# Some float32r operands begin 64 bytes past a multiple of 128 instead of at one

## The chip, the cores and the metric

The kernel runs as one program on one core of a Trainium2 chip. The metric is the device time of one execution in microseconds (us); the median of several executions is what counts. TensorE (PE) does the matrix products, its weight loads are listed on their own as PEld, VectorE is DVE, ScalarE is ACT, GpSimd is POOL, and SP issues the transfers from HBM.

## The reference, cut to what matters

Two blocks of two layers each work on 256 tokens of width 1024, all in float32:

```python
# first block, layer i = 0, 1
h = mixer_block(h, ...)          # rmsnorm, u @ w_in (1024 x 9232), retention, gated delta rule, two branches, w_out
u = rmsnorm(h, norm_ffn[i])
h = h + swiglu(u, ...)           # layer 0: (silu(u @ wg) * (u @ wu)) @ wd, width 2816
h = h + moe(u, ...)              # layer 1: 8 experts of width 1408, two for each token
h = h + sigmoid(rmsnorm(h, norm_ple[i]) @ w_ple_gate[i]) * (p[i] @ w_ple[i])
# second block, layer 0: hgrn2 mixer, layer 1: dilated attention, each followed by
u = rms_norm(h, norm_g[layer, 2]) * (1.0 + sc2) + sh2
y = swiglu_ffn(u, ffn_w_in[layer], ffn_w_out[layer])     # width 2816
```

Nearly all arithmetic is a product of normed activations with a weight matrix that is read once.

## The kernel before, in words

Each float32 product is made of three float32r products. A value is split into a high part, rounded to float32r, and a low part, the rest; `high*high`, `high*low` and `low*high` are summed in PSUM. For the weights, `fetch` brings 1 MB (128 partitions x 2048 floats) into a buffer `raw`, ACT writes the high part `whi` and DVE the low part `wlo` (`parts`, lines 241 to 263 of the file), two tiles of 1024 columns of each. For the activations, `norm` writes `uh` and `ul`, which live in the constant pool for the whole program and hold 8 blocks of 256 tokens; `split_out` writes the others: `ro` (retention output), `go` (delta-rule output), `ma` (the merged branches), `fh`/`fl` (the hidden layer of a dense FFN), `ho`, `ao`, and in the experts `x`, `y`, `hh`, `hl`.

There are two forms of the product. In `ws_block` the weights are the stationary operand (128 x 128) and the activations move, 256 columns (256 tokens) at a time: three matmuls for each of the 8 blocks of the inner dimension. In `ts_tile` a 128 x 128 block of the activations is stationary and the weights move, 256 columns in `tok` and `toks`, 272 in `gdn_gates`, 384 or 512 in the output projections and the experts. The trace names the moving operand first and the stationary one second: `pg<-uh,whi` is a matmul into `pg` that moves `uh` over the stationary `whi`. Every matmul has a weight load of its own. The order of PE's instructions is the order in which the program is written (a manual schedule for PE); the other engines are ordered by the planner, and a matmul waits only for its operands and for its PSUM tile.

Where a tile lies is decided by the order of first use. A pool is a stretch of each partition's SBUF; inside it every tag gets its buffers at the place where the tag is first asked for, rounded to 32 bytes. The class `Even` wraps a pool: it counts the bytes given so far (`at`) and, before a new tag of type float32r (or one of a few float32 tags that share their place with one), it inserts an unused tile `pad`, so that the tag begins at a multiple of 128 bytes. It pads the end of each pool in the same way, so the next pool begins at a multiple of 128. In the kernel before, the addresses (bytes within a partition) come out so:

| tile | address | modulo 128 | modulo 256 |
|---|---|---|---|
| `h` (8192 bytes, ends at 27840) | 19648 | 64 | 192 |
| `uh`, `ul` (8192 bytes each) | 27904, 36096 | 0 | 0 |
| last tile of the constant pool, 64 bytes | 50016 | 96 | 96 |
| `raw` (3 x 8192 bytes), then `whi`, `wlo` (4 x 4096 bytes each) | 50176, 74752, 91136 | 0 | 0 |
| `go`, four buffers in the mixer's pool | 128512 and up (layer 1: 151552) | 0 | 0 |
| `ro`, `ma`, two shared buffers of the tag `A` | 212096, 220288 | 0 | 128 |
| `fh`, `fl` in the dense FFN | 134656, 157184 | 0 | 0 |
| `ho` and `ao` | 169344 and up, 185984 and up | 0 | 128 |

A block of the inner dimension is 1024 bytes of `uh` and 1024 bytes of a weight tile with 256 columns, so within a tile all operands begin at the same place modulo 256. The one exception is `gdn_gates` (output `pgz`): its weight tile has 272 columns, 1088 bytes, so of the two blocks in a tile the first begins at 0 and the second at 64 modulo 128.

Of the kernel before, what the change touches and what calls it, by code (L numbers as in the profile page):

```python
# [7 lines left out]
F32 = mybir.dt.float32  # L8
F32R = mybir.dt.float32r
# [35 lines left out]
class Even:  # L45
# [3 lines left out]
    def __init__(self, pool, bufs):  # L49
        self.pool, self.bufs, self.at, self.tags, self.pads = pool, bufs, 0, set(), 0  # L50

    def even(self):
        if self.at % 128:
            n = (128 - self.at % 128) // 4
            self.pads += 1
            self.pool.tile([128, n], F32, tag=f"pad{self.pads}", name="pad", bufs=1)
            self.at += 4 * n

    def tile(self, shape, dt, tag=None, name=None, bufs=None):
        if tag is None:  # L60
            tag = name
        if tag not in self.tags:
            if dt == F32R or tag in ("raw", "rawo", "uq", "A", "y", "whi", "wlo"):
                self.even()
            self.tags.add(tag)
            size = 2 if dt == BF16 else 4
            for n in shape[1:]:
                size *= n
            self.at += -(-size // 32) * 32 * (bufs or self.bufs)
        return self.pool.tile(shape, dt, tag=tag, name=name, bufs=bufs or self.bufs)  # L70


@contextmanager
def even_pool(tc, name, bufs, **k):
    with tc.tile_pool(name=name, bufs=bufs, **k) as pool:
        p = Even(pool, bufs)
        yield p
        p.even()
# [6 lines left out]
class Net:  # L85
# [23 lines left out]


    @contextmanager
    def phase(self, name, n, nsplit=0):

        tp = lambda name, bufs: even_pool(self.tc, name, bufs, reuse_waits="tile")
        with ExitStack() as st:
            self.php = pool = st.enter_context(tp(name, 1))
            if n:
                self.ap = st.enter_context(tp(name + "_a", n))
            if nsplit:
                st.enter_context(self.more_weights(0, nsplit))  # L120
            yield pool
# [21 lines left out]
            self.tick()  # L143

    def A(self, name, dt=F32):
        return self.ap.tile([128, 2048], dt, tag="A", name=name)

    def psm(self, name="pm"):
        return self.mm.tile([128, 512], F32, tag="mm", name=name)
# [29 lines left out]
    def setup(self, p):  # L179
        nc = self.nc  # L180
        i = self.i
        self.cst = self.cp.tile([128, NCONST, 128], F32, name="cst")
        nc.sync.dma_start(self.cst[:, 0, :], i["cst"][:, 0, :])
        self.ident = self.cst[:, C_ID, :]
        self.M = self.cst[:, C_M, :]
        self.nhalf = self.cp.tile([128, 16], F32, name="nhalf")
        nc.vector.memset(self.nhalf, -0.5)
        self.ones = self.cp.tile([128, 128], F32, name="ones")
        nc.vector.memset(self.ones, 1.0)
        self.h = self.cp.tile([128, 2, D], F32, name="h")  # L190
        self.u = tuple(self.cp.tile([128, 2048], F32R, name=n) for n in ("uh", "ul"))

    def columns(self, items, new):

# [261 lines left out]
    def mixer(self, l, nxt):  # L456
# [2 lines left out]
        w = self.w3(i["w_in"][l])  # L459
        rq, rk, rv, rg, gq, gk, gv, gz, mgr, mgg = 0, 512, 1024, 2048, 3072, 4096, 5120, 6144, 7184, 8208  # L460
        u, tile = self.next
        with self.phase("mix", 2) as mp:
            self.mp = mp
            self.hold = True
            ret_a = self.pair("ro")
# [184 lines left out]
    def gdn_chain(self, l, p, qkv, st):  # L650

        mp = self.mp
        H = 2 * p
        qs, ks, vs = qkv
        pn = self.pss("pn")
        for j, x in enumerate((qs, ks)):
            sq = mp.tile([128, 2, T], F32, tag="cacc", name="sq2", bufs=2)
            self.act(sq, x, AF.Square)
            yield
            yield  # L660
            for h in range(2):
                for t in range(2):
                    n = t * 4 + j * 2 + h
                    self.mmul(pn[:, n:n + 1], sq[:, h, t * 128:(t + 1) * 128], self.ones[:, 0:1])
        ms = mp.tile([128, 2, 2, 2], F32, tag="gms", name="gms", bufs=2)
        r = mp.tile([128, 2, 2, 2], F32, tag="grn", name="grn", bufs=2)
        self.ts(ms.rearrange("p a b c -> p (a b c)"), pn[:, :8], 4 * EPS, None, OP.add)
        self.pow(r.rearrange("p a b c -> p (a b c)"), ms.rearrange("p a b c -> p (a b c)"), 8)
        hv = mp.tile([128, 2, 2], F32, tag="ghv", name="ghv", bufs=2)
        self.stt(hv, ms[:, :, 1, :], 0.5, r[:, :, 1, :], OP.mult, OP.mult)  # L670
        bp = mp.tile([128, 2, 2], F32, tag="gbp", name="gbp", bufs=2)
        self.tt(bp, r[:, :, 1, :], r[:, :, 1, :], OP.mult)
        self.tt(bp, bp, self.g_beta[:, :, H:H + 2], OP.mult)
        fq = mp.tile([128, 2, 2], F32, tag="gfq", name="gfq", bufs=4)
        self.ts(fq, r[:, :, 0, :], 128.0 ** -0.5)
        uq = mp.tile([128, 1536], F32, tag="uq", name="uq", bufs=4)
        U, Q = (uq[:, 768 * n:768 * (n + 1)].rearrange("p (h n i) -> p h n i", h=2, n=3) for n in range(2))
        pr, dc = {}, {}

        def decay(h):  # L680
            hh = H + h
            pr = self.pss("pr")
            g0 = self.g_g[:, 0, hh:hh + 1].to_broadcast([128, 128])
            g1 = self.g_g[:, 1, hh:hh + 1].to_broadcast([128, 128])
            self.mmul(pr[:, 0:128], g0, self.M, start=True, stop=False)
            self.mmul(pr[:, 0:128], self.idb, self.negb, start=False, stop=True)
            self.mmul(pr[:, 128:384], g1, self.M[:, None, :].to_broadcast([128, 2, 128]))
            self.mmul(pr[:, 256:384], self.idb, self.negb, start=False, stop=True, skip=True)
            dc[h] = mp.tile([128, 3, 128], F32, tag="dc", name="dc", bufs=2)
            for n in range(3):  # L690
                self.act(dc[h][:, n, :], pr[:, n * 128:(n + 1) * 128], AF.Exp, bias=self.g_bias[:, n, hh:hh + 1])

        decay(0)
        pv = self.pss("pv")
        for t in range(2):
            for h in range(2):
                self.tr(pv[:, (t * 2 + h) * 128:(t * 2 + h + 1) * 128], vs[:, h, t * 128:(t + 1) * 128])
        vt = mp.tile([128, 2, 2, 128], F32, tag="vt", name="vt", bufs=4)
        for t in range(2):
            for h in range(2):  # L700
                n = t * 2 + h
                self.act(vt[:, t, h, :], pv[:, n * 128:(n + 1) * 128], AF.Identity, scale=hv[:, t, h:h + 1])
        if p % 2 == 0:
            self.Uc = mp.tile([128, 8, 32], F32, tag="Uc", name="Uc", bufs=2)
        for h in range(2):
            yield
            for x, dst in ((ks, U), (qs, Q)):
                pg = self.pss("pg")
                self.mmul(pg[:, 0:256], ks[:, h, 0:128], x[:, h, :])
                self.mmul(pg[:, 256:384], ks[:, h, 128:256], x[:, h, 128:256])  # L710
                self.stt(dst[:, h, 0:2, :], pg[:, 0:256].rearrange("p (a b) -> p a b", b=128), bp[:, 0, h:h + 1],
                         dc[h][:, 0:2, :])
                self.stt(dst[:, h, 2, :], pg[:, 256:384], bp[:, 1, h:h + 1], dc[h][:, 2, :])
            if not h:
                decay(1)
            for g in range(4):
                r = slice(32 * g, 32 * g + 32)
                n = 4 * (p % 2) + 2 * h
                self.act(self.Uc[r, n:n + 2, :], U[r, h, 0:3:2, r])
        st[p] = U, Q, vt, fq  # L720

    def gdn_out(self, l, st, begun, then, sgz, p, ga):
        mp = self.mp
# [23 lines left out]
        for h in range(2):  # L747
            self.mmul(po[:, h * 128:(h + 1) * 128], Q[:, h, 0, :], z[:, 0, h, :])
            self.mmul(po[:, (2 + h) * 128:(3 + h) * 128], Q[:, h, 1, :], z[:, 0, h, :], start=True, stop=False)
            self.mmul(po[:, (2 + h) * 128:(3 + h) * 128], Q[:, h, 2, :], z[:, 1, h, :], start=False, stop=True)  # L750
        o = mp.tile([128, 1536], F32R, tag="uq", name="go", bufs=4)
        o = o[:, :512], o[:, 512:1024]
        while p not in sgz:
            yield
# [948 lines left out]
def begin(net):  # L1703
# [8 lines left out]
    cols = net.columns([(n, r2(i[n])) for n in ("norm_mix", "norm_ffn", "norm_ple", "ret_gn")],  # L1712
                       lambda: net.tp.tile([128, 512], F32, tag="th", name="colrow", bufs=2)[:, :128])
# [7 lines left out]
    def loads():  # L1721
# [5 lines left out]
        items = [("gdn_gn", i["gdn_gn"]), ("c", r2(i["c"])), ("hgrn_norm_g", r2(i["hgrn_norm_g"])),  # L1727
                 ("lower", r2(i["hgrn_lower_bounds"]))]
        items += [(f"conv{l}", i["conv_w"][l].rearrange("w (r p) -> (w r) p", p=128)) for l in range(2)]
        items += [("ada_b", r2(i["ada_b"])), ("norm_g", i["norm_g"].rearrange("l n (r p) -> (l n r) p", p=128))]  # L1730
        cols = net.columns(items, lambda: net.mp.tile([128, 1536], F32, tag="uq", name="colrow", bufs=4)[:, :128])
        net.dtb, net.nea = [], []
        for l in range(2):
            a = cp.tile([128, 8], F32, name=f"nea{l}")
# [113 lines left out]
```

## Time and the profile before

| | us |
|---|---|
| median of 3 runs (2305.77 to 2308.68) | 2306.74 |
| the profiled execution, its own time | 2304.72 |
| its span, from the first to the last instruction | 2302.8 |
| PE busy | 2230.3 (97%) |
| DVE busy | 1695.0 (74%) |
| ACT busy | 1283.6 (56%) |

A span is one execution as the hardware profiler saw it; the execution's own time holds 1.9 us more around it. Matmuls are pipelined, and each is listed with its latency: one of 256 columns shows 0.28 us although the next begins 0.12 us later. So neither the busy share nor the duration of a matmul tells what it costs; the distance between the starts of successive matmuls does.

### The profile page before, as it was taken

To read this page: it belongs to the slowest core of one execution; us is meant where nothing else is said; L and a number is where in the kernel's file an instruction comes from. 1 tells how busy PE (TensorE), PEld (TensorE's weight loads), DVE (VectorE), ACT (ScalarE), POOL (GpSimd) and SP (SyncE) were. 2 spreads that over 40 slices of the span, in tenths; PEclk is the share of its full clock that TensorE was granted. 3 is DMA by queue.
4 is the path that set the end of the run, shared out by engine and by line. 5 is a ranking of instruction groups with operands and counts; after the bars stand their busy time and mean duration, and the time that the engine had idled before them with its cause. 6 is when DMAs were issued, how large, how long until landed. Compare 5 with 4: busy or idle time off the path is not lost.

```text
span 2302.8 us, 38609 instructions
## 1 busy us (share of the span) xinstructions
PE 2230.3 (97%) x15571; PEld 2070.6 (90%) x15571; DVE 1695.0 (74%) x2596; ACT 1283.6 (56%) x1992; POOL 169.3 (7%) x142
## 2 busy tenths in 40 slices
PE   8999999999999999989999999989999999999998
PEld 7998998998899899978888887887998899998997
DVE  6878667766687885679999997786777666666554
ACT  5655445433566444468787776654543555456443
POOL 0032100000003210000000000331000000000000
PEclk9999999999999999999999999999999999999999
DMA  7443566876454355769999996434677554444553
GB/s 233 147 133 127 185 218 209 280 253 250 150 182 138 103 179 194 245 223 369 318 358 339 319 342 218 131 122 146 229 267 269 198 176 137 149 145 138 182 176 135
DMA packets 338525, 478.57 MB, mean 208 GB/s; under 512 B 9874, under 2 KB 239116, under 8 KB 338340
## 3 DMA queue, kind: packets, MB, share of 16 engines
q1 hardware_dynamic: 338340, 476.05, 61.3%
q8 instruction: 123, 2.02, 0.4%
q14 instruction: 62, 0.51, 0.1%
HBM read 474.95 MB, written 1.06 MB: 207 GB/s over the span
## 4 chain that ended last, share of the span: by engine, by line
issue 31%; PE 20%; DVE 3%; POOL 1%; ACT 1%; POOLq 0%; DVEq 0%; ACTq 0%
PE peg L170 5%; PE peu L170 5%; PE pey L170 5%; DVE wlo L158 1%; PE pgat L170 1%; PE phg L170 1%; PE po L170 1%; PE phq L170 1%; PE pho L170 1%; POOL ms L345 0%; PE psc L170 0%; POOL rs L176 0%; PE pht L173 0%; PE phv L170 0%; ACT whi L155 0%
## 5 line engine op out<-in xcount | busy, mean ns | idle before, releaser
L158 DVE TENSOR_TENSOR wlo<-raw,whi 128x1024 fp32r<-128x1024 f32 (+2 forms) x802 | 929.5, 1178 | 310.3 <-ACT whi L155 303.9
L155 ACT ACTIVATE whi<-raw 128x1024 fp32r<-128x1024 f32 (+3 forms) x828 | 832.6, 1022 | 531.2 <-PE po L170 57.3
L170 PE MATMUL pu<-uh,whi 128*128 128x256 f32 x480 | 136.3, 284 | 0.0
L170 PE MATMUL pg<-uh,whi 128*128 128x256 f32 x480 | 136.0, 283 | 0.0
L170 PE MATMUL pg<-ul,whi 128*128 128x256 f32 x480 | 135.8, 283 | 0.0
L170 PE MATMUL pg<-uh,wlo 128*128 128x256 f32 x480 | 135.8, 283 | 0.0
L170 PE MATMUL pu<-ul,whi 128*128 128x256 f32 x480 | 135.8, 283 | 0.0
L170 PE MATMUL pu<-uh,wlo 128*128 128x256 f32 x480 | 135.8, 283 | 0.0
L345 POOL TENSOR_SCALAR ms<-ss 128x1 f32<-128x1 f32 x30 | 16.4, 548 | 1498.7 <-ACT junk L155 1498.7
L167 DVE SCALAR_TENSOR_TENSOR acc<-raw,cond,acc 128x1024 f32<-128x1024 f32 x84 | 108.3, 1289 | 18.0 <-DMA raw<-in_ada_w_dram 17.2
L170 PE MATMUL paq<-uh,whi 128*128 128x256 f32 x384 | 112.3, 293 | 0.0
L170 PE MATMUL pqkv<-uh,whi 128*128 128x256 f32 x384 | 110.2, 287 | 0.0
L170 PE MATMUL pqkv<-uh,wlo 128*128 128x256 f32 x384 | 108.8, 283 | 0.0
L170 PE MATMUL paq<-uh,wlo 128*128 128x256 f32 x384 | 108.7, 283 | 0.0
L170 PE MATMUL pqkv<-ul,whi 128*128 128x256 f32 x384 | 108.6, 283 | 0.0
L170 PE MATMUL paq<-ul,whi 128*128 128x256 f32 x384 | 108.6, 283 | 0.0
L170 PE MATMUL po<-whi,fh 128*128 128x512 f32 x264 | 103.2, 391 | 1.1 <-DVE fm L167 1.1
L170 PE MATMUL po<-wlo,fh 128*128 128x512 f32 x264 | 103.0, 390 | 0.7 <-DVE wlo L158 0.7
L170 PE MATMUL po<-whi,fl 128*128 128x512 f32 x264 | 102.8, 389 | 0.0
L170 PEld LDWEIGHTS pg<-uh,whi 128*128 128x128 f32 x480 | 92.1, 192 | 0.9 <-ACT fh L155 0.9
L170 PEld LDWEIGHTS pu<-uh,whi 128*128 128x128 f32 x480 | 92.1, 192 | 0.9 <-ACT whi L155 0.9
L170 PEld LDWEIGHTS pg<-uh,wlo 128*128 128x128 f32 x480 | 92.1, 192 | 0.0
(470 smaller groups left out, 6587.6 us busy)
## 6 DMA issues: line engine op xcount, KB each, us to landing
raw<-in_w_in_dram SPq DMA_DIRECT2D x70, 1024.0 KB
raw<-in_ada_w_dram SPq DMA_DIRECT2D x48, 1024.0 KB
raw<-in_ffn_w_in_dram SPq DMA_DIRECT2D x44, 1024.0 KB
raw<-in_attn_w_in_dram SPq DMA_DIRECT2D x36, 1024.0 KB
raw<-in_exp_w_gate_dram SPq DMA_DIRECT2D x32, 1024.0 KB
raw<-in_exp_w_up_dram SPq DMA_DIRECT2D x32, 1024.0 KB
raw<-in_exp_w_down_dram SPq DMA_DIRECT2D x32, 1024.0 KB
raw<-in_ffn_w_out_dram SPq DMA_DIRECT2D x20, 1024.0 KB
```

The source lines that it names most:

```text
L155: self.nc.scalar.activation(out, in_, func, scale=scale, bias=bias, **k)
L158: self.nc.vector.tensor_tensor(out, a, b, op=op)
L167: self.nc.vector.scalar_tensor_tensor(out, a, s, b, op0=op0, op1=op1)
L170: self.nc.tensor.matmul(out, lhsT, rhs, start=start, stop=stop, skip_group_check=skip)
L345: self.nc.gpsimd.tensor_scalar(ms, self.ss[:, t, 0:1], self.ss[:, t, 1:2], EPS, op0=OP.add, op1=OP.add)
```

## The change: what it does, and the diff

`Even.even` and `Even.tile` take a flag `odd`: with it a tag begins at 64 modulo 128 instead of 0. It is set for four tags: `uh` and `ul` in the constant pool, the tag `A` of the mixer's phase (`ro`, then `ma`), and the tag `uq` (`go`, the delta rule's float32 blocks `uq`, and a scratch tile `colrow`). All other tags stay at multiples of 128. The flag is passed through `phase` and kept in `self.odd`, which `A` reads. No instruction is added, removed or reordered by the text of the diff, and no tile changes its size; only pads and addresses change.

```diff
-    def even(self):
-        if self.at % 128:
-            n = (128 - self.at % 128) // 4
+    def even(self, odd=False):
+        n = (64 * odd - self.at) % 128 // 4
+        if n:
             self.pads += 1
             self.pool.tile([128, n], F32, tag=f"pad{self.pads}", name="pad", bufs=1)
             self.at += 4 * n
...
             if dt == F32R or tag in ("raw", "rawo", "uq", "A", "y", "whi", "wlo"):
-                self.even()
+                self.even(odd)
...
-        return self.ap.tile([128, 2048], dt, tag="A", name=name)
+        return self.ap.tile([128, 2048], dt, tag="A", name=name, odd=self.odd)
...
-        self.u = tuple(self.cp.tile([128, 2048], F32R, name=n) for n in ("uh", "ul"))
+        self.u = tuple(self.cp.tile([128, 2048], F32R, name=n, odd=True) for n in ("uh", "ul"))
...
-        with self.phase("mix", 2) as mp:
+        with self.phase("mix", 2, odd=True) as mp:
...
-        uq = mp.tile([128, 1536], F32, tag="uq", name="uq", bufs=4)
+        uq = mp.tile([128, 1536], F32, tag="uq", name="uq", bufs=4, odd=True)
...
-        o = mp.tile([128, 1536], F32R, tag="uq", name="go", bufs=4)
+        o = mp.tile([128, 1536], F32R, tag="uq", name="go", bufs=4, odd=True)
```

## Rows read from the trace of the kernel before

**Rows 1.** The page's head: span, busy time, the granted clock in 40 slices.

```profile
span 2302.8 us, 38609 instructions
...
PE 2230.3 (97%) x15571; PEld 2070.6 (90%) x15571; DVE 1695.0 (74%) x2596; ACT 1283.6 (56%) x1992; POOL 169.3 (7%) x142
...
PEclk9999999999999999999999999999999999999999
```

**Rows 2.** Stages: length; PE, PEld, DVE, ACT, POOL busy; clock, DMA share, GB/s.

```profile
380.00:515.00 135.00, 133.98 (x1100) 131.61 (x1099) 105.55 (x122) 62.85 (x85) 1.24 (x2) 1.00 0.79 259
982.00:1453.00 471.00, 455.47 (x2211) 385.30 (x2211) 418.98 (x518) 351.69 (x457) 6.30 (x10) 0.98 0.86 304
1837.00:2065.00 228.00, 228.00 (x1856) 225.98 (x1855) 145.94 (x200) 117.05 (x168) 0.00 (x0) 1.00 0.48 156
```

**Rows 3.** Timeline of PE, attention: first and last of 190 successive matmuls.

```profile
1839.72 0.28 PE L170 MATMUL paq<-uh,wlo 128*128 128x256 f32 x1
...
1862.40 0.28 PE L170 MATMUL paq<-uh,wlo 128*128 128x256 f32 x1
```

**Rows 4.** The same, experts: first and last of 21 matmuls of 384 columns.

```profile
1035.88 0.33 PE L170 MATMUL peu<-whi,xh 128*128 128x384 f32 x1
...
1039.35 0.33 PE L170 MATMUL peu<-whi,xl 128*128 128x384 f32 x1
```

**Rows 5.** The same, FFN's output projection: first and last of 58 matmuls of 512 columns.

```profile
532.01 0.39 PE L170 MATMUL po<-whi,fh 128*128 128x512 f32 x1
...
544.93 0.39 PE L170 MATMUL po<-whi,fh 128*128 128x512 f32 x1
```

**Rows 6.** Timeline of PE: weight loads of sixteen one-column matmuls, and the next load.

```profile
300.22 1.86 PEld L170 LDWEIGHTS pmod<-ones,acc 128*128 128x128 f32 x16
302.01 0.19 PEld L170 LDWEIGHTS py<-roh,whi 128*128 128x128 f32 x1
```

**Rows 7.** Timeline of PE: retention branch, first and last of 23 successive matmuls.

```profile
270.41 0.28 PE L170 MATMUL py<-rol,whi 128*128 128x256 f32 x1
...
273.03 0.28 PE L170 MATMUL py<-roh,wlo 128*128 128x256 f32 x1
```

**Rows 8.** Timeline of PE: mixer's output projection, first and last of 64 successive matmuls.

```profile
357.13 0.39 PE L170 MATMUL po<-whi,mal 128*128 128x512 f32 x1
...
371.77 0.39 PE L170 MATMUL po<-whi,mal 128*128 128x512 f32 x1
```

**Rows 9.** Timeline of PE: `gdn_gates`, first and last of 34 successive matmuls.

```profile
32.87 0.29 PE L170 MATMUL pgz<-whi,ul 128*128 128x272 f32 x1
...
36.99 0.29 PE L170 MATMUL pgz<-whi,ul 128*128 128x272 f32 x1
```

**Rows 10.** Matmuls of the whole span by operand: `uh`, `ul`, `go` (PE busy, count).

```profile
0.00:2303.00 2303.00, 1189.19 (x6272) 0.99 0.62 208
0.00:2303.00 2303.00, 901.40 (x3168) 0.99 0.62 208
0.00:2303.00 2303.00, 47.06 (x384) 0.99 0.62 208
```

**Rows 11.** Groups by line and shape, PE: the other counts (one of three parts each).

```profile
L170 PE MATMUL py<-roh,whi 128*128 128x256 f32 x128 | 37.4, 292 | 0.0
L170 PE MATMUL po<-whi,mah 128*128 128x512 f32 x64 | 25.6, 400 | 0.0
L170 PE MATMUL po<-whi,uh 128*128 128x512 f32 x64 | 25.6, 399 | 0.5 <-ACT uh L155 0.5
L170 PE MATMUL pgat<-P,uh 128*128 128x256 f32 x64 | 13.8, 300 | 5.6 <-PEq L1030 5.6
L170 PE MATMUL pgz<-whi,uh 128*128 128x272 f32 x32 | 9.4, 294 | 0.0
```

**Rows 12.** Groups by line and shape, DVE and ACT: the split of the weights.

```profile
L158 DVE TENSOR_TENSOR wlo<-raw,whi 128x1024 fp32r<-128x1024 f32 x702 | 847.0, 1223 | 290.6 <-ACT whi L155 284.9 <-issue 0.2
L155 ACT ACTIVATE whi<-raw 128x1024 fp32r<-128x1024 f32 x728 | 758.3, 1057 | 488.1 <-PE po L170 57.3 <-PE paq L170 45.6 <-issue 45.6
```

More of the change, by code (lines that the diff above doesn't have):

```diff
@@ L57, in even, with tile @@
             self.at += 4 * n
-    def tile(self, shape, dt, tag=None, name=None, bufs=None):
+    def tile(self, shape, dt, tag=None, name=None, bufs=None, odd=False):
         if tag is None:
@@ L111, in phase @@
     @contextmanager
-    def phase(self, name, n, nsplit=0):
+    def phase(self, name, n, nsplit=0, odd=False):
         tp = lambda name, bufs: even_pool(self.tc, name, bufs, reuse_waits="tile")
         with ExitStack() as st:
+            self.odd = odd
             self.php = pool = st.enter_context(tp(name, 1))
@@ L1730, in loads @@
         items += [("ada_b", r2(i["ada_b"])), ("norm_g", i["norm_g"].rearrange("l n (r p) -> (l n r) p", p=128))]
-        cols = net.columns(items, lambda: net.mp.tile([128, 1536], F32, tag="uq", name="colrow", bufs=4)[:, :128])
+        cols = net.columns(items, lambda: net.mp.tile([128, 1536], F32, tag="uq", name="colrow", bufs=4, odd=True)[:, :128])
         net.dtb, net.nea = [], []
```

## The prediction

> **What bounds the kernel now.** I read the page's head first, then the stages, then the starts of single matmuls. [...] The stages say where that share means something: in the dense FFN PE is busy 133.98 of 135 us and in the attention layer 228.00 of 228, while DVE, the next engine, has 105.55 and 145.94 there [rows 2]. In the experts PE shows 455 of 471 us, but there DVE (419) and the transfers (0.86 of the DMA engines' time) press as well; the change hardly touches that stage. So a change of the distance between two matmuls goes into the time nearly whole. A busy share can't show that distance, the starts can. In the attention layer 190 matmuls of 256 columns stand 22.68 / 189 = 0.1200 us apart [rows 3]; with 384 columns it is 3.47 / 20 = 0.1735 [rows 4], with 512 columns 12.92 / 57 = 0.2267 [rows 5]. [...] What is left, 120.0 - 106.7 = 13.3 ns, is the same for all three shapes: a fee for each matmul, whatever its length. It is all that an address can act on. The reader should see that it is constant: not one matmul in those stretches escapes it.
>
> **What the change does, part by part.** It adds and removes no instruction and no transfer, and moves nothing in any queue. What changes are distances between operands. Before, `h` ends at 27840 and 64 bytes of pad follow. Now `uh` begins at 27840 itself, everything behind it in the constant pool lies 64 lower, that pool ends at 50016, padded to 50048, and the weights' tiles begin at 74624 instead of 74752. Modulo 256, `uh` is at 192 and the weights at 128: activations minus weights goes from 0 to 64. All later pools move down by 128 together, so `fh`, `x`, `hh`, `ho` and `ao` keep their distance to the weights. In the mixer's pool of layer 0 `go` goes from distance 0 to 64 and `ro`/`ma` from 128 to 64; layer 1's `go` gets 64 or 192.
>
> Counts: matmuls that read `uh` or `ul` are 6272 + 3168 = 9440, those with `go` 384 [rows 10], those with `ro` 3 x 128 = 384 [rows 11]. Of the 9440, 3 x 32 are `pgz`, 3 x 64 are 512-column products of the PLE gate, and 2 x 64 are the experts' gather [rows 11]; 9024 remain with 256 columns, with `go` 9408. They all stood at distance 0.
>
> The price of distance 64 for such a matmul is not in the trace of before. The bounds: it can't gain more than the fee, and not all of that, since the weight loads need time of their own. Sixteen loads in a row for one-column matmuls take 1.79 / 16 = 0.112 us each [rows 6], so 256 columns can come down from 120 to 112, by 8.0 ns, and 9408 of them with the 384 of `ro` by 78 us. In the other direction the nearest row is the mixer's output projection: at distance 128 its 512-column matmuls stand 14.64 / 63 = 232.4 ns apart instead of 226.7, 5.7 ns worse [rows 8]; on all 9408 that would be 54 us.
>
> Between the bounds two rows are near. The retention branch moves `ro` at distance 128 over 256 columns: 2.62 / 22 = 119.1 ns, 0.9 better than at distance 0 [rows 7]. So the same distance hurts at 512 columns and helps a little at 256. And `gdn_gates` is the only place where float32r operands stand 64 apart at all, in every second block: its 272 columns should take 272 x 0.417 + 13.3 = 126.7 ns and take 4.12 / 33 = 124.8, 1.8 less [rows 9]. If only the blocks at 64 gain, that is 3.6 ns for each of those. I take the middle between 0.9 and 3.6, 2.25 ns, because the first row has the right shape at another distance and the second the right distance in half its blocks.
>
> The sum: 9408 x 2.25 = 21.2 us off; `ro` already has 0.9 of it, 384 x 1.35 = 0.5 us off; the PLE gates' 192 matmuls of 512 columns leave distance 0, and I charge them the 5.7 ns of [rows 8], 1.1 us on; `ma` stays off distance 0 and keeps its price; `pgz` and the gather are 224 matmuls, 0.5 us either way, left at nothing. Together 20.6 us off the profiled execution's 2304.7: 2284.1. That execution lies 2.0 us under the median of the runs, so the forecast in the median's terms is 2286.
>
> [...]
>
> Edits that I cost at nothing: ACT and DVE now write `uh`, `ul`, `ro`, `go`, `ma` 64 bytes further on, and no row shows such a write apart; PE covers it, as ACT is busy 56% and DVE 74% [rows 1]. If PE gets faster, the weights' split comes next: 48 matmuls of one pass last 5.76 us and need two splits, 2 x 1.223 us of DVE and 2 x 1.057 of ACT [rows 12]; at 2% less that still fits. The transfers in the dense FFN would go from 0.79 to 0.81 of the DMA engines' time.
>
> **The rivals.** *Nothing happens.* The fee is one of any float32r matmul, and the starts only shuffle it: within 0.2% of 2307. For it: the fee is exactly the same for three shapes, and 1.8 ns in `pgz` is little. Against it: [rows 7 to 9] all depart from the fee, and they are the only stretches quoted whose distance isn't 0.
>
> *The fee goes nearly away.* At 64 the matmuls settle near the loads' limit: 78 us off, 2229, or some 2244 at four fifths of it. For it: `pgz` has only every second block at 64, so its pattern never settles. Against it: its mean is 124.8, and the retention branch, always off distance 0, stays at 119.1.
>
> *It gets slower.* Place: the 256-column passes over `uh`. [...] Price: up to 5.7 ns on each, 2361; at a third of it, 2325. It decides from 4.6 / 9408 = 0.5 ns a matmul. For it: distance 0 holds one constant value, and every other distance is irregular; a pattern that the rows don't contain may be bad. Against it: the 256-column row off distance 0 is better than the fee, and so is `pgz`.
>
> *The change doesn't do what it says.* The addresses follow from sizes alone, so this I give no chance beyond the first rival's.
>
> **How the numbers follow.** The forecast, 5 to 45 us off, has 0.50; a larger gain 0.18; nothing 0.15; slower 0.17. 0.2% of the time, 4.6 us, is about what a measurement of this kernel can tell from no change. Faster is 0.50 + 0.18 = 0.68, same 0.15, slower 0.17. The range reaches to 2240, which takes in the larger gain but for its last part (0.05 left out), and up to 2312, which leaves out the slower cases of more than 0.6 ns a matmul (0.12). The forecast's own range is 2262 to 2302.
>
> **What would show it.** In the changed kernel's timeline the stretch of attention matmuls: a distance of about 117.7 ns where 120.0 stands, with an irregular or shorter repeating pattern; `py<-roh` and `py<-go` alike; `po<-whi,uh` slower than 226.7 ns, `po<-whi,fh` and the experts exactly as before. Wrong is the forecast if the 256-column distance stays 120.0 (then the first rival), if it comes to 113 or less, if it goes above 120, or if the matmuls get closer and the gain is lost again to waits for `wlo` or for transfers.

## The result and the profile after

| | before | changed |
|---|---|---|
| median of 4 runs each, us | 2306.26 (2303.81 to 2308.68) | 2281.03 (2278.66 to 2284.09) |
| ratio, with 95% interval | | 0.9891 [0.9874, 0.9909] |
| profiled execution, us | 2304.72 | 2284.09 |

Faster by 25.2 us in the median (forecast: 2286) and by 20.6 us between the two profiled executions (forecast: 20.6). The head of the changed kernel's page, to be held against [rows 1]:

```profile
span 2282.2 us, 38609 instructions
...
PE 2205.0 (97%) x15571; PEld 2044.7 (90%) x15571; DVE 1694.3 (74%) x2596; ACT 1282.9 (56%) x1992; POOL 170.0 (7%) x142
...
PEclk9999999999999999999999999999999999999999
```

The instructions are the same in number, DVE, ACT and POOL are busy as long as before. Only PE became shorter, by 25.3 us. Its idle time (span less PE) grew from 72.5 to 77.2 us.

The digits of the granted clock show whole tenths over long slices, so a row of 9 doesn't say that it was 1.00 throughout. The means of the two profiled executions differ, and neither is 1:

```profile
core 0: 2302.8 us, clock 0.992
...
core 0: 2282.2 us, clock 0.989
```

The granted clock has two levels in both traces, 1.00 and 0.50; PE was at the lower one for 38.4 us of the first and 49.0 us of the second. The time follows this share here: over 56 executions of the kernel before, the median is 2304.2 us where the mean clock was 0.992 (10 of them) and 2308.4 where it was 0.989 (11). The changed kernel's four had 0.989 to 0.993; each held against the kernel before at its own clock is 23 to 24 us faster. The 20.6 us of the profiled pair are about 3 us short of that, because the two had different clocks.

The stage table shows the attention layer as full as in [rows 2]; it is only that less time goes by in it:

```profile
1837.00:2065.00 228.00, 228.00 (x1845) 223.69 (x1845) 150.89 (x214) 121.01 (x177) 0.00 (x0) 1.00 0.48 158
```

So the starts must be read again. The timeline of PE of the changed kernel; each pair is the first and last matmul of one unbroken stretch:

```profile
1835.76 0.28 PE L171 MATMUL paq<-ul,whi 128*128 128x256 f32 x1
...
1870.15 0.28 PE L171 MATMUL paq<-uh,wlo 128*128 128x256 f32 x1
...
935.05 0.28 PE L171 MATMUL py<-go,wlo 128*128 128x256 f32 x1
...
945.93 0.28 PE L171 MATMUL py<-go,wlo 128*128 128x256 f32 x1
...
268.83 0.28 PE L171 MATMUL py<-rol,whi 128*128 128x256 f32 x1
...
271.42 0.28 PE L171 MATMUL py<-roh,wlo 128*128 128x256 f32 x1
...
585.09 0.40 PE L171 MATMUL po<-whi,uh 128*128 128x512 f32 x1
...
604.46 0.39 PE L171 MATMUL po<-whi,ul 128*128 128x512 f32 x1
...
354.28 0.40 PE L171 MATMUL po<-wlo,mah 128*128 128x512 f32 x1
...
373.05 0.40 PE L171 MATMUL po<-whi,mal 128*128 128x512 f32 x1
...
529.74 0.39 PE L171 MATMUL po<-whi,fh 128*128 128x512 f32 x1
...
571.67 0.39 PE L171 MATMUL po<-whi,fl 128*128 128x512 f32 x1
```

- Attention: 293 matmuls, 34.39 / 292 = 117.8 ns, against 120.0 in [rows 3]. The single distances go through 117, 118 and 119 in a fixed turn.
- Delta-rule branch of layer 1: 97 matmuls, 10.88 / 96 = 113.3 ns. This is a second steady value, 113, 113, 114, and it was not forecast.
- Retention branch: 23 matmuls, 2.59 / 22 = 117.7 ns, against 119.1 in [rows 7]; other passes of the same loop run at 113.3.
- PLE gate: 84 matmuls of 512 columns, 19.37 / 83 = 233.4 ns, against 226.7 in [rows 5].
- Mixer's output projection: 83 matmuls, 18.77 / 82 = 228.9 ns, better than the 232.4 of [rows 8].
- Dense FFN's output projection, distance still 0: 186 matmuls, 41.93 / 185 = 226.6 ns, as in [rows 5]. The experts' 384 columns still take 173.4 ns ([rows 4]: 173.5), and `pgz` 124.7 on the mean ([rows 9]: 124.8).

To hold this against the forecast's sum, the distance from each matmul's start to the next was taken over the whole trace. A column more takes (226.7 - 120.0) / 256 = 0.417 ns in [rows 3] and [rows 5]. Where a distance is more than 8% above (columns x 0.417 + 15) ns, its excess over that sum was put aside; the other distances were averaged by group:

| group | matmuls | forecast, ns each | before, ns | changed, ns | us in all |
|---|---|---|---|---|---|
| 256 columns, `uh`/`ul` move over the weights | 6,720 | -2.25 | 119.9 | 117.3 | -17.4 |
| 256 columns, weights move over `uh`/`ul` | 2,304 | -2.25 | 119.8 | 115.6 | -9.8 |
| `go` | 384 | -2.25 | 119.9 | 115.6 | -1.6 |
| `ro` | 384 | -1.35 | 118.9 | 115.9 | -1.2 |
| PLE gate, 512 columns | 192 | +5.7 | 227.6 | 233.2 | +1.1 |
| `ma`, 512 columns | 192 | 0 | 232.4 | 229.1 | -0.7 |

These rows make -29.6 us; over all matmuls the distances fall from 2046.2 to 2017.5 us (-28.7), and what was put aside grows from 243.2 to 252.1 us (+8.9). Not all of that is waiting. Where the clock is at its lower level (0.50) the matmuls themselves are far apart, as after this wait for `wlo` in the changed kernel (a row of the stages, then the timeline of PE):

```profile
1508.50:1512.50 4.00, 4.00 (x21) 4.00 (x21) 4.00 (x2) 2.82 (x4) 3.32 (x1) 0.50 0.82 259
```

```profile
1508.61 0.41 PE L171 MATMUL phg<-whi,uh 128*128 128x256 f32 x1
...
1512.66 0.41 PE L171 MATMUL phg<-wlo,uh 128*128 128x256 f32 x1
```

20 matmuls, 4.05 / 19 = 213.2 ns, which is 0.83 ns a column, twice 0.417. In the stretches at that level 44 matmuls of 256 columns or more stood so before and 87 in the changed kernel, 3.9 of the 8.9 us. That leaves 5.0 us of waits, and the page agrees in its own terms (idle time +4.7). So the change gave more in distances than was forecast, and about a sixth of it came back as waits.

Which waits grew is seen in the view of PE's waits. Before (sum, times, longest):

```profile
PE pn L170 <- DVE diag L162: 13.5, 7, 3.5
...
PE phg L170 <- DVE wlo L158: 4.9, 1, 4.9
...
PE py L170 <- DVE go L167: 2.3, 2, 1.1
PE pz L170 <- DVE vt L158: 2.2, 2, 1.3
PE pav L170 <- DVE wlo L158: 1.8, 1, 1.8
...
PE po L170 <- DVE fm L167: 1.1, 1, 1.1
```

and of the changed kernel:

```profile
PE pn L171 <- DVE diag L163: 14.5, 8, 3.3
...
PE phg L171 <- DVE wlo L159: 5.4, 1, 5.4
...
PE pav L171 <- DVE wlo L159: 2.7, 2, 1.8
PE py L171 <- DVE go L168: 2.6, 2, 1.4
...
PE po L171 <- DVE fm L168: 2.0, 1, 2.0
```

These are places where PE stood behind DVE already before. With the 2.2 and 2.9 us of `pz` behind `vt`, the six come from 25.8 to 30.1 us, and all that this view puts down to DVE from 38.6 to 43.4: DVE is no faster, PE gets there earlier.

### The profile page after: what moved, and what is told of

Read it like the earlier page. It is cut to its first block, busy times and chain, and to the rows that moved or that the text cites. A ratio compares the mean times of both kernels' runs of the same rounds, so it can differ in the third digit from the quotient of the medians.

```text
span 2282.2 us, 38609 instructions
## 1 busy us (share of the span) xinstructions
PE 2205.0 (97%) x15571; PEld 2044.7 (90%) x15571; DVE 1694.3 (74%) x2596; ACT 1282.9 (56%) x1992; POOL 170.0 (7%) x142
## 4 chain that ended last, share of the span: by engine, by line
issue 31%; PE 21%; DVE 2%; POOL 1%; ACT 1%; POOLq 0%; DVEq 0%; ACTq 0%
PE peg L171 5%; PE peu L171 5%; PE pey L171 5%; DVE wlo L159 1%; PE phg L171 1%; PE pgat L171 1%; PE pf L171 1%; PE po L171 1%; PE phv L171 1%; PE phq L171 1%; PE pho L171 1%; POOL ms L346 0%; PE psc L171 0%; POOL rs L177 0%; PE pht L174 0%
```

## The experiments

**The price by itself.** In the traces only the distance had changed on purpose, but the pools had moved too, and DVE, ACT and the transfers are busy at the same time (145.94 us, 117.05 us and 0.48 in the attention layer's 228 us [rows 2]). A kernel with nothing but matmuls takes all that away:

```diff
+ for d in range(0, 256, 16):            # activations U begin d bytes past the weights W, modulo 256
+     series(f"A{d}", "ws", d, 0, 2)     # 2 x 2 x 24 matmuls of 256 columns: (wh,uh) (wh,ul) (wl,uh)
+ series("Aeq", "ws", 64, 64, 2); series("Ash", "ws", 128, 64, 2); series("Aneg", "ws", 0, 64, 2)
+ for d in range(0, 256, 32): series(f"T{d}", "ts256", d, 0, 1)   # 48 matmuls, the weights move
+ for d in range(0, 256, 32): series(f"F{d}", "ts512", d, 0, 1)
```

> This kernel leaves the whole network out and measures the disputed price by itself: stretches of 96 matmuls of 256 columns with the kernel's own order of three parts, one stretch for each distance (activations minus weights) from 0 to 240 bytes in steps of 16, then the output projections' form with 256 and with 512 columns, steps of 32; nothing else runs beside them. Theory (the distance of the two starts sets the spacing): 120.0 ns at distance 0; at 64 the values of the changed kernel, 117.9 or 113.3; both operands moved by 64 together give 120.0 again; activations at 128 over weights at 64 give the same as 64 over 0; 512 columns 226.7 at distance 0 and 232 to 234 at 64 and 128. Rival, place alone (a start at 64 modulo 128 is good by itself): both moved by 64 together give 113 to 118, not 120. Rival, neighbours (the spacing comes from DVE, ACT and the transfers using SBUF at the same time): all distances alike here, spread under 1 ns. Open: whether another distance gives 113.3 throughout.

Timeline of PE; a row is a whole series (start, length, count). The names lose their number; in order of time these are A0, A64, A96, A112, A192, then Aeq, Ash, T64, F0, F64 and F192:

```profile
26.86 11.78 PE L45 MATMUL A<-U,W 128*128 128x256 f32 x96 [0.69 <-ACT sink L57]
...
75.89 11.57 PE L45 MATMUL A<-U,W 128*128 128x256 f32 x96 [0.75 <-ACT sink L57]
...
100.75 11.77 PE L45 MATMUL A<-U,W 128*128 128x256 f32 x96 [0.75 <-ACT sink L57]
113.27 11.20 PE L45 MATMUL A<-U,W 128*128 128x256 f32 x96 [0.75 <-ACT sink L57]
...
174.71 11.19 PE L45 MATMUL A<-U,W 128*128 128x256 f32 x96 [0.75 <-ACT sink L57]
...
223.73 11.78 PE L45 MATMUL Aeq<-U,W 128*128 128x256 f32 x96 [0.75 <-ACT sink L57]
236.25 11.15 PE L45 MATMUL Ash<-U,W 128*128 128x256 f32 x96 [0.75 <-ACT sink L57]
...
273.51 5.73 PE L54 MATMUL T<-W,U 128*128 128x256 f32 x48 [0.75 <-ACT sink L57]
...
313.46 11.22 PE L54 MATMUL F<-W,U 128*128 128x512 f32 x48 [0.75 <-ACT sink L57]
...
337.64 11.48 PE L54 MATMUL F<-W,U 128*128 128x512 f32 x48 [0.75 <-ACT sink L57]
...
386.50 11.27 PE L54 MATMUL F<-W,U 128*128 128x512 f32 x48 [0.75 <-ACT sink L57]
```

The distances differ, 113.3 to 120.0 ns for 256 columns, with no other engine at work (DVE, ACT and POOL are busy for 0.00 us in the windows of the A and F series), so the rival "neighbours" falls. Both operands moved by 64 (Aeq) cost what distance 0 costs (11.78 us for the 96), so "place alone" falls too. And what counts here is moving minus stationary: where the weights move, the row for activations at 64 (T64) is like A192 (113.3 ns), and where 512 columns move, 64 is the dearer (233.3 ns) and 192 the cheaper (228.9). The means over each series' second half, by moving minus stationary:

| moving minus stationary | 0 | 16 | 32 | 48 | 64 | 80 | 96 | 112 | 128 | 144 | 160 | 176 | 192 | 208 | 224 | 240 |
|---|---|---|---|---|---|---|---|---|---|---|---|---|---|---|---|---|
| 256 columns, ns | 120.0 | 113.3 | 116.7 | 118.3 | 117.8 | 120.0 | 120.0 | 113.3 | 118.6 | 116.7 | 118.6 | 119.2 | 113.3 | 119.2 | 118.3 | 117.2 |
| 512 columns, ns | 226.7 | | 233.3 | | 228.9 | | 233.3 | | 232.1 | | 234.5 | | 233.3 | | 233.3 | |

The row of 256 columns is from the series in which the activations move; the eight distances at which the weights moved gave the same within 0.2 ns. Each value is that of one series, and at 16, 64, 144 and 192 another series took another value (below). One thing missed the expectation: A64 and Ash stand at the same distance and took 117.8 and 113.3.

**Either part alone.** `u_only` takes the flag from the mixer's tags, `mix_only` takes it from `uh` and `ul`:

```diff
- with self.phase("mix", 2, odd=True) as mp:      # u_only; also without odd=True for uq, go, colrow
+ with self.phase("mix", 2) as mp:
...
- self.u = tuple(... name=n, odd=True) for n in ("uh", "ul"))     # mix_only
+ self.u = tuple(... name=n) for n in ("uh", "ul"))
```

> Only the normed activations at 64, the mixer's two tags at multiples of 128 again. Theory (9,024 of the 256-column matmuls move or hold the normed activations, 384 the delta rule's output, 384 the retention's): nearly all of the gain, 23 to 25 us off the kernel before, 2282 to 2284; branch of the delta rule back at 120.0 ns. Rival (part of the gain comes from the mixer's scheduling, its chains ending earlier with the float32 blocks at other places): less than 20 us off.

> Only the mixer's two tags at 64, the normed activations at a multiple of 128 again. Theory: 384 x (120.0 - 117.9 or 113.3) for the delta rule's output, 384 x (119.1 - 117.9 or 113.3) for the retention's and 192 x 3.4 for the merged branches: 2 to 5 us off, 2301 to 2304. Rival (mixer's share is larger): 7 us off or more.

Measured: `u_only` 2288.15 us, ratio 0.9915 [0.9901, 0.9928], 18.5 us off; `mix_only` 2301.96 us, 0.9980 [0.9971, 0.9989], 4.6 us off. `mix_only` came out as its theory said. `u_only` fell short of 23 to 25 us, as its rival said, but not for the rival's reason: the distances fell by 27.2 us, and 15.5 us more were put aside, 5.3 of them matmuls at the lower clock (this execution's mean clock was 0.987). Of its six executions, five can be held against the kernel before at the same clock; they are 18 to 25 us faster. The mixer's own part is small (3.4 us in distances). The two times add up to 23.1 of the 25.2 us, and the spacings are as expected: with `u_only` the delta-rule branch is back at 119.9 ns and `ma` at 232.4, with `mix_only` the attention layer is at 120.0.

`u_only` also shows the second state in the network. In the stretch of [rows 3], at the same distance 64 as in the changed kernel, its timeline of PE has

```profile
1837.46 0.28 PE L171 MATMUL paq<-uh,whi 128*128 128x256 f32 x1
...
1878.15 0.28 PE L171 MATMUL paq<-uh,wlo 128*128 128x256 f32 x1
```

360 matmuls, 40.69 / 359 = 113.3 ns, where the changed kernel had 117.8.

**Two states at one distance.** The second map enters four distances four times each, behind a matmul of another length, and tries 512 and 384 columns at more distances:

```diff
+ for d in (64, 192, 16, 112):
+     for lead in (64, 144, 200, 250): series(f"A{d}_{lead}", "ws", d, 0, 2, lead)
```

> Leaves the network out again. In the first map the repeating state of a stretch was set by moving minus stationary start modulo 256: 192 gave 113.3 ns in both forms, 64 gave 117.8 in one stretch of either form and 113.3 in another. Here each of the distances 64, 192, 16 and 112 is entered four times, each time behind one matmul of another length (64, 144, 200, 250 columns), then 512 columns at the odd multiples of 16, 384 columns at all multiples of 16, and 256 columns at distances that are only multiples of 8. Theory (the distance alone decides which states exist, the way in decides which of them is taken where there are two): 192 gives 113.3 in all four, 64 gives both 113.3 and 117.8 among its four. Rival (the distance and the absolute place together decide, each pair has one state): all four alike at every distance, 64 at 117.8. For 512 columns no theory gives numbers; if the 256-column states carry over, one of the odd multiples of 16 is below 226.7.

Timeline of PE: the first of the four series at 64, then all four at 192:

```profile
27.43 11.55 PE L47 MATMUL A<-U,W 128*128 128x256 f32 x96
...
77.16 11.15 PE L47 MATMUL A<-U,W 128*128 128x256 f32 x96
...
89.23 11.52 PE L47 MATMUL A<-U,W 128*128 128x256 f32 x96
...
101.69 11.07 PE L47 MATMUL A<-U,W 128*128 128x256 f32 x96
...
113.72 11.06 PE L47 MATMUL A<-U,W 128*128 128x256 f32 x96
```

The theory had the numbers the wrong way round. It was 192 that took two values, 113.3, 117.8, 113.3 and 113.3, although no address differs among the four. All four at 64 took 117.8, all four at 112 took 113.3, and those at 16 took 116.7 or 118.7 where the first map had 113.3. At 512 columns no distance tried beat the 226.7 ns of distance 0, at 384 none its 173.4 by more than 0.1.

The third map sets the way in against the place: distance 64 at eight places, 112 and 192 at four, all of it twice.

```diff
+ for turn in range(2):
+     for base in (0, 32, 64, 96, 128, 160, 192, 224): series(f"A{base}", "ws", base + 64, base, 2)
+     for base in (0, 64, 128, 192): series(f"B{base}", "ws", base + 112, base, 2)
+     for base in (0, 64, 128, 192): series(f"C{base}", "ws", base + 192, base, 2)
+ for k in range(4): series(f"D{k}", "ts256", 112, 0, 1, 64 + 60 * k)
```

> The network left out again. Distance 64 at eight absolute places 32 bytes apart, distances 112 and 192 at four places 64 apart, all of it twice; then the form that moves the weights with the activations 112 and 64 bytes past them, four ways in each. Theory (the distance sets which repeating states there are, the way in sets which one is taken, the place sets nothing): distance 64 shows 117.8 and now and then 113.3 at any place, and a place that shows 113.3 in the first turn need not in the second; 112 stays at 113.3 at every place; 192 shows both. Rival (the place chooses): the same places show 113.3 in both turns, 128 over 64 among them, which did in the first map. For the weights moving: 116.7 or 118.7 with activations at 112 (moving minus stationary 144), 113.3 mostly at 64 (192).

All sixteen at 64 took 117.8 and all eight at 112 took 113.3. At 192 the places gave 117.8, 117.8, 113.3, 113.3 in the first turn and 117.8, 117.8, 117.8, 113.3 in the second. The third place, in both turns:

```profile
198.46 11.17 PE L47 MATMUL C<-U,W 128*128 128x256 f32 x96 [0.75 <-ACT sink L60]
...
393.24 11.57 PE L47 MATMUL C<-U,W 128*128 128x256 f32 x96 [0.74 <-ACT sink L60]
```

The same addresses, two prices: the place doesn't choose. But in both turns the matmuls ahead are the same too, so the length of the matmul ahead isn't shown to choose either. The network has such a pair as well: 97 successive matmuls of layer 1 (`pqkv`) stand 113.3 ns apart in the profiled execution of the changed kernel (636.15 to 647.03 us) and 117.8 in that of the same program run again (`after_again` below, 633.10 to 644.40 us). Over the three maps 64 gave 117.8 in 22 series of 23, 192 gave 113.3 in 12 of 19, 112 gave 113.3 in 13 of 13. With the weights moving and the activations at 112 (moving minus stationary 144) the mean was 120.0 in all four, not the 116.7 expected; whether 144 too has two states or the two forms differ there is open. With the activations at 64 (192) it was 113.3 in three series of four, as expected.

**The network at other distances.** All tags now go by multiples of 256, the four tags at a distance `OFF`, the HGRN2 and attention outputs at 0:

```diff
- def even(self, odd=False):
-     n = (64 * odd - self.at) % 128 // 4
+ def even(self, off=0):
+     n = (off - self.at) % 256 // 4
...
+ OFF = 192        # u192;  u96: 96;  u0: 0
...
+ self.u = tuple(self.cp.tile([128, 2056], F32R, name=n, off=96)[:, 4:2052] for n in ("uh", "ul"))   # u112
```

> The whole network; places now go by multiples of 256: the four tags of the change begin 192 bytes past the weights' place instead of 64, and the outputs of the HGRN2 and attention layers move from distance 128 to distance 0. No work is left out. Theory (moving minus stationary decides): the 6,272 matmuls that move uh, ul come from mostly 117.9 to 113.3 ns, 25 us off; the some 2,900 that move weights over them go from 113.3 or 117.9 to 117.8 or 113.3, between 5 us off and 10 us on; PLE gates from 233.3 to 228.9 and 384 matmuls of the two output projections from 232.4 to 226.7, 3 us off together. Sum 18 to 33 us off the changed kernel: 2248 to 2263. Rival (64 and 192 are alike, the sign doesn't count): 2278 to 2281. Rival (PE is no longer the bound below 117 ns, the split of the weights or the transfers come next): spacing 113.3 in the trace, but less than 12 us off.

> The same with 96 bytes, a distance off zero that the map says is worth nothing to the form that moves the activations: 120.0 ns on the mean, in a pattern of 124, 118, 121, 117, 125, 115. The form that moves the weights stands at 160 then, 118.8 in the map; PLE gates at 512 columns 233 to 235; the two layers' output projections at 226.7. No work is left out. Theory (moving minus stationary decides, as mapped): 120.0 in the attention layer, 3 to 6 us off the kernel before, 2300 to 2303. Rival (anything but distance 0 breaks the slow pattern): 10 us off or more. Rival (the pools' new places bring the time): as much off as with 192.

> Control: the same code with the four tags at distance 0, so that every pool lies where it lies in these versions, but all operands begin at the same place modulo 256; only the HGRN2 and attention outputs, the retention's and the merged branches come from 128 to 0. No work is left out. Theory: 120.0 ns everywhere again, 384 + 192 matmuls of 512 columns from 232.4 to 226.7 ns, 3.3 us off the kernel before, 2302 to 2304. Rival (the new places of the pools bring part of the time): more than 8 us off.

> The same as the run with 192 bytes, except that uh and ul stand 112 bytes past the weights' place instead of 192; no work is left out. In both maps distance 112 gave 113.3 ns in the form that moves the activations, behind every one of its five ways in, while 192 fell into 113.3 or 117.8. In the form that moves the weights, moving minus stationary is then 144, 116.7 in the map. Theory (a distance with one state gives it in the network too): the 6,272 matmuls that move uh, ul at 113.3 throughout (117.9 for half of them at 192), the 2,900 others at 116.7; spacing alone 10 to 16 us less than at 192, of which a third comes back as waits as it did there: 2268 to 2274. Rival (in the network the way in is always new, so there are two states at 112 as well): 113.3 in about half the stretches and 2278 to 2284.

| | us, median | ratio to before, 95% | `uh`/`ul` move, ns | weights over `uh`/`ul`, ns | distances / put aside, us |
|---|---|---|---|---|---|
| before | 2306.7 | | 119.9 | 119.8 | 2046.2 / 243.2 |
| `u0` | 2306.0 | 0.9999 [0.9986, 1.0012] | 119.9 | 119.8 | 2044.9 / 244.3 |
| `u96` | 2305.7 | 0.9994 [0.9982, 1.0006] | 119.9 | 118.0 | 2043.3 / 246.5 |
| `u192` | 2280.7 | 0.9886 [0.9866, 0.9906] | 115.3 | 117.2 | 2005.5 / 258.0 |
| `u112` | 2278.1 | 0.9877 [0.9859, 0.9896] | 114.0 | 119.9 | 2004.1 / 258.6 |

The stretch of [rows 3] in `u96`, then in `u112`:

```profile
1839.93 0.28 PE L172 MATMUL paq<-uh,whi 128*128 128x256 f32 x1
...
1883.01 0.28 PE L172 MATMUL paq<-uh,wlo 128*128 128x256 f32 x1
```

```profile
1825.29 0.28 PE L172 MATMUL paq<-uh,whi 128*128 128x256 f32 x1
...
1865.98 0.28 PE L172 MATMUL paq<-uh,wlo 128*128 128x256 f32 x1
```

360 matmuls each: 43.08 / 359 = 120.0 ns at 96, in the map's uneven pattern (116, 123, 118, 121, 117, 125), and 40.69 / 359 = 113.3 at 112. `u96` is the strongest test: off zero, with all pools moved, and worth nothing, as the map has it. `u0` moves the pools as well and is worth nothing, so the pools' places didn't bring the time. Both stayed short of the few microseconds expected of their 512-column matmuls: the distances fell by 1.3 and 2.9 us, what was put aside grew by 1.1 and 3.3.

`u192` failed its expectation of 2248 to 2263. The distances fell 12.0 us under the changed kernel's (2017.5), but with a mean of 115.3 ns and not 113.3; what was put aside grew by 5.9, and the median is no better. That speaks for the rival "PE is no longer the bound", but the clock has a part in it: `u192` ran at 0.984 to 0.992, the changed kernel at 0.989 to 0.993. Where both had the same clock, `u192` took 2270.9 us at 0.992 and 2278.0 at 0.989, the changed kernel 2281.2 and 2284.1, so something of the 12.0 us did reach the time.

`u112` has the steady 113.3 in the attention layer that was expected, 42.1 us less in distances than before, of which 15.4 were put aside again, 4.1 of them at the lower clock. Its 2278.1 us missed the 2268 to 2274 expected and lies in its rival's range, though not for the rival's two states at 112: the weights that move over `uh`/`ul` at 144 took 119.9 ns instead of 116.7, so its distances are only 1.4 us under those of `u192` and not 10 to 16.

**The two best, on the same chip.** `after_again` is the changed kernel, `best` is `u112` with `go` at 112 too:

```diff
- o = o[:, :512], o[:, 512:1024]
+ o = o[:, 4:516], o[:, 516:1028]      # the tag uq at 96, so go begins at 112
```

> The changed kernel as it is, beside the next one on the same chip, for a comparison of the two. 2278 to 2284.

> The 112-byte version with the delta rule's output at 112 as well (before: 192); no work is left out. Theory: its 384 matmuls come from 113.3 or 117.8 to 113.3, under 1 us; the sum of spacings stays near 42 us under the kernel before, of which some 15 us return as waits for DVE's chains: 2274 to 2280, 2 to 6 us under the changed kernel. Rival (the waits take all that lies beyond the changed kernel's gain): the same as the changed kernel within 2 us.

Measured: `after_again` 2285.59 us (2280.64 to 2285.74), 0.9901 [0.9884, 0.9917]; `best` 2274.50 us (2271.69 to 2281.85), 0.9864 [0.9840, 0.9887]. The first lies 1.6 us above its range, the second in its range of 2274 to 2280. By the medians `best` is 11.1 us under the changed kernel (2 to 6 were expected) and 31.5 under the one before; the two intervals just touch, and against the changed kernel's first four executions (2281.03) it is 6.5, so a gain over the changed kernel is likely, its size not certain. The waits of `best`, for three of the places above:

```profile
PE phg L172 <- DVE wlo L160: 5.6, 1, 5.6
...
PE po L172 <- DVE fm L169: 4.5, 2, 2.9
...
PE py L172 <- DVE go L169: 3.1, 2, 1.8
```

These three have grown once more: PE reaches `fm`, the product in the FFN's hidden layer, `go` and `wlo` earlier than DVE has them ready (behind `diag` and `vt` it waits less than in the changed kernel, 13.3 and 1.9 us). All that was put aside is 258.0 us against 243.2 before, 4.6 of the difference at the lower clock. Some of that follows the longer waits: in the dense FFN's output projection of `best` PE waits 2.90 us for `fm` up to 508.3 us, and from 508.9 to 515.7 us the granted clock is 0.50, where the kernel before had 1.00 (505 to 530 us).

## Why the prediction was right, and where it was not

*"The fee is all that an address can act on"* held. The 106.7 ns are what 256 columns more take, 226.7 ([rows 5]) - 120.0 ([rows 3]), and no distance tried came below them: the shortest, 113.3 ns, is 106.7 + 6.7, and 120.0 is 106.7 + 13.3. So it is half the fee that a distance took away at most, for 256 columns; for 512 columns none of the distances tried was better than 0 (226.7 ns).

*The price of distance 64, 2.25 ns from the middle of two rows,* was right for its largest group (2.6 on 6,720) and mis-sized for the others (4.2 on 2,304 with the weights moving, 4.3 on `go`). The step that failed is that one price was taken for one distance: over the activations the moving weights stand at -64, which is 192, and so does `go` in layer 1 over its weights (the prediction names "64 or 192" there and charges both alike). At 192 a part of the stretches falls into the faster state; the mean of 115.6 lies midway between 113.3 and 117.8. No row of before could tell, since there all of them stood at 0.

*"`ro`/`ma` go from 128 to 64"* was wrong. The sign was lost: both come to lie 64 bytes short of the weights' place, at 192. For `ro` that is the distance with two states (3.0 ns gained instead of 1.35), and for `ma`, which is stationary, the weights move at +64, which costs 228.9 in the map and 229.1 here. The step "`ma` keeps its price" fell with it; both together are 1.3 us.

*The PLE gate, charged 5.7 ns,* took 5.6. `pgz`, the experts and the dense output projections stayed, as forecast.

*"At 2% less that still fits"*, the claim that PE would cover all else, failed in part: about 5 us came back as waits behind DVE, at places where PE already waited. Of the 4.3 us that the six rows above gained, 1.4 are for the weights' split (`wlo`), to which the claim was tied, and 2.9 for `diag`, `go`, `vt` and `fm`. In the profiled execution the distances gave 8.1 us more than the sum; 5.0 went to these waits and 3.9 to the lower clock, which the digits of [rows 1] don't show. These nearly cancel, so that the sum met the 20.6 us of this pair of executions is luck. At equal clock the gain is 23 to 24 us, and the sum is 3 us short.

Of the rivals, *nothing happens* fell with the starts: one and the same shape took 120.0 ns with both operands at one place and 113.3 or 117.8 at 64 and 192; what is behind it, no run shows. *The fee goes nearly away* didn't come either; half of it stayed in the best state. Its floor holds, though: 113.3 lies 1.3 ns above the 112 of the loads alone [rows 6]. *It gets slower* was right for the PLE gate alone (5.6 ns).

Two things stay open. Why these distances and not others: the runs give a table, not a mechanism. And what selects the state: the same program with the same addresses took either, in the map and in the network, so it is neither the place nor the code ahead alone.

## What to carry to other kernels

When the busy share is near 100%, read the starts of single matmuls: a constant fee, here the same 13.3 ns for three shapes, is a candidate for something cheap to move. Measure such a price in a kernel that does nothing else, over all distances and both directions, before choosing one; here 16 bytes more or less (96 against 112) decided between nothing and the whole gain, and the choice of 64 gave two thirds of what the distances had to give (28.7 of 43.1 us in `best`). And price the waits of the engines behind: of what the last versions took out of the distances beyond the changed kernel (12.0 to 14.4 us), 40 to 50% came back as waits or as matmuls at the lower clock. And before two executions are compared to a few microseconds, compare their mean granted clocks: here 0.992 against 0.989 was worth 4 us.

## What the runs showed of the hardware

In the maps and the networks of this case a stretch of float32r matmuls, each with a weight load, settles into a repeating pattern whose mean goes with moving minus stationary start modulo 256: 113.3 to 120.0 ns for 256 columns, 173.3 to 177.5 for 384, 226.7 to 234.5 for 512. Some distances have more than one (192 and 64: 113.3 and 117.8; 16: 113.3, 116.7 and 118.7), and the same program can take either. A stretch keeps the one that it fell into: no unbroken stretch of 48 or more matmuls of 256 columns with `uh`/`ul` in the changed kernel went from one to the other while the same operand moved, and the longest has 911 (117.8 ns). Distances that were multiples of 8 only (8, 24, 40, 56, 184, 200) were no better, 118.3 to 120.0 ns.

At the lower granted level (0.50) the matmuls of 256 columns stand 213 ns apart and those of 512 columns 426 to 427, so a column takes 0.83 ns and no fee is left: at distance 0 in the kernel before (`phg`) as at 192 in the changed one (`phg`, and 427 for two of the PLE gate). The fee of 6.7 to 13.3 ns was seen at the level 1.00 only.
